# First stage of a two-layer trunk: x first, a smaller first modulation, and a fixed order of issue

## The chip, the cores and the metric

The kernel runs on one NeuronCore of one Trainium2 chip. The metric is the device time of one execution in microseconds (us); a lower time is better. Five kinds of work appear in the profile: PE (TensorE, matrix products, with its weight loads listed as PEld), DVE (VectorE), ACT (ScalarE), POOL (GpSimd) and SP (SyncE), which here issues all transfers between the chip's main memory (HBM) and the on-chip memory (SBUF). PE writes its results to PSUM, from which DVE and ACT read them.

## The reference, cut to what matters

The input `x` has 1024 tokens of 1024 channels, `c` is one conditioning vector. There are two layers, each of the form

```
mod = silu(c) @ ada_w[l] + ada_b[l]
shift, scale, gate = split(mod, 3)
h = rms_norm(x, norm_g[l]) * (1 + scale) + shift
x = x + gate * mixer(h)
```

with `rms_norm(x, g) = x * rsqrt(mean(x * x) + 1e-6) * g` over the channels of a token. The first layer's mixer begins with a projection `h @ w_in` into 3072 channels: q, k, v and a gate of a differential attention, and `x_b` and a gate of a recurrent unit that starts with a convolution of `x_b` along the tokens. The second layer is a neighbourhood attention. A final norm follows.

The change touches only the beginning: the modulation of layer 0, its `rms_norm`, `h`, and the first three slabs (128 output channels each) of the projection.

## The kernel before, in words

**Layout.** Channels lie on the 128 partitions and tokens along the free dimension, so `x` is eight chunks `k` of 128 channels by 1024 tokens. The tokens are worked in two halves `hf` of 512. `half(k, hf)` is one such tile, 128 x 512, 256 KB.

**Exact products.** A product of two 32-bit operands is made of three matmuls: each operand is split into a high part and a remainder (`whi`, `wlo` for a weight slab, `ahi`, `alo` for `h`), and hi·hi, lo·hi and hi·lo are added up in PSUM. A weight slab `i` is a tile `raw` of 512 KB; `split_next` (L159) copies it on ACT into `whi` (L185) and subtracts on POOL for `wlo` (L186), and then loads the next slab (`load_next`, L151).

**The stage before the change** (L503 to L608) does this:

- `squares(hf)` (L516) loads the eight tiles of one half of x, squares them on ACT, some on DVE, and sums the squares over the channels on PE with a matrix of ones (`ss_add`, L366). Each sum is four narrow matmuls, 32 columns of PE each, one for every 128 tokens.
- `mod_first(g)` (L266) loads the modulation weights of two chunks of channels (group `g` of four; eight tiles of 256 KB), sums them on PE with silu(c) as the weight (`sums`, again four narrow matmuls a tile), copies the row on ACT (L296), turns it into a column with a small matmul (L298), and makes `gain` (1 + scale times the norm's gain) and the shift on DVE (L302, L304).
- `scale(hf)` (L539) makes 1/sqrt(mean + eps) on DVE with a bit trick and three Newton steps (`rstd_rows`, L371), spreads it over all partitions with four matmuls (`spread`, L395) and copies it to SBUF on ACT.
- `parts(g, hf)` (L547) calls `make_h` (L399) for two chunks: DVE multiplies x by gain and rstd (L404), ACT adds the shift and rounds to the high part (L405), DVE makes the remainder (L406).
- `products(i, g, hf)` (L553) adds two chunks of one half into slab i's bank: 2 x 3 matmuls of 512 columns (L563, L564, L565). Three slabs, two halves, eight chunks: 144 matmuls in all.
- `small_constants` (L463) is a chain of small DVE steps for the recurrent unit and the attention's lambda, with a Tanh and an Exp on ACT. It is called at the start.

**What sets the order.** A scheduler places each engine's instructions: by their order in the program, among those that it takes to be ready by its own estimates. `tc.high_priority()` moves instructions ahead; `tc.issue_after(ins)` places what is in its block behind `ins` on the same engine's queue, without a wait for its end. Once placed, an engine runs its queue in order, SP's transfers too. In the kernel before, x's first half is loaded first, then the first modulation group, then x's second half, then groups 1, 2 and 3, with the slabs between.

**What follows the stage.** `evac_xb` (L411) copies slabs 0 and 1 from PSUM on ACT; `conv` (L693) works on them on ACT and DVE (L699, L707, L712, L717). `gate_w` (L722) loads and splits the gates' weights (L727 on ACT, L728 on POOL). Meanwhile the job list that begins at L841 runs on PE: half a projection of slab 3, 24 matmuls (`proj`, L201 to L203), and then by turns three gate matmuls on the convolution's result and six matmuls of further projections, with a sigmoid on ACT after every gate.

Of the kernel before, what the change touches and what calls it, by code (L numbers as in the profile page):

```python
# [97 lines left out]
def kernel(ctx, tc, xT, xTp, small, lamp, adaw, tb, w0, gw, wo0, w1, nab, wo1, out):  # L98
# [100 lines left out]

    def mm3(ps, lh, ll, rh, rl, start, stop):  # L200
        T.matmul(ps, lh, rh, start=start, stop=False)  # L201
        T.matmul(ps, lh, rl, start=False, stop=False)  # L202
        state["pe"] = T.matmul(ps, ll, rh, start=False, stop=stop).ins  # L203
# [62 lines left out]
    def mod_first(g, pool, small, c32):  # L266

        ps = ptp.tile([P, HF], F32, tag="pt", name=f"mod{g}")

        def sums(x, w, start, stop):  # L270
            for n in range(4):
                cols = x[:, n // 2, (n % 2) * P:(n % 2 + 1) * P]
                state["modmm"] = T.matmul(ps[32 * n:32 * n + 32, :P], w, cols,
                                          start=start, stop=stop)

        pieces = []
        for k in range(KC):
            where, tag, bufs = pool, "ada", KC
            if g % 2:
                where, tag, bufs = kqp, ("qq0", "qq1", "qlo")[k // 3], 3  # L280
            piece = where.tile([P, 2, 2 * P], F32, tag=tag, name="ada", bufs=bufs)
            src = adaw[0, k * P:(k + 1) * P, :2 * D].rearrange("p (t n) -> p t n", t=2)
            state["ada"] = nc.sync.dma_start(piece[:], src[:, :, 2 * g * P:(2 * g + 2) * P])
            pieces.append(piece)
        if g == 0:
            for k in range(KC):
                sums(pieces[k], c32[:, k, :], k == 0, k == KC - 1)
        else:

            with tc.high_priority():  # L290
                sums(pieces[KC - 1], c32[:, KC - 1, :], True, False)
                with tc.issue_after(state["modmm"].ins):
                    for k in range(KC - 1):
                        sums(pieces[k], c32[:, k, :], False, k == KC - 2)
        row = pool.tile([P, P], F32, tag="mrow", name="mrow", bufs=2)
        A.activation(row[:], ps[:, :P], AF.Copy)  # L296
        pc = ps[:, P:]
        T.matmul(pc[:, :4], row[:], pick[:], start=True, stop=True)  # L298
        m = small.tile([P, 2, 2], F32, tag=f"first{g}", name=f"first{g}", bufs=1)
        gain = small.tile([P, 2], F32, tag=f"gain{g}", name=f"gain{g}", bufs=1)  # L300
        b = sm[:, O_ADAB:O_ADAB + 2 * KC].rearrange("p (t k) -> p t k", t=2)
        V.tensor_tensor(m[:], pc[:, :4].rearrange("p (t j) -> p t j", t=2),  # L302
                        b[:, :, 2 * g:2 * g + 2], ALU.add)
        V.scalar_tensor_tensor(gain[:], m[:, 1, :], 1.0, sm[:, O_NG + 2 * g:O_NG + 2 * g + 2],  # L304
                               ALU.add, ALU.mult)
        for j in range(2):
            first_mod[2 * g + j] = gain[:, j:j + 1], m[:, 0, j:j + 1]
# [58 lines left out]
    def ss_add(ss, sq, start, stop, w=P):  # L366
# [28 lines left out]
    def spread(rr, bc, w=P):  # L395
# [3 lines left out]
    def make_h(l, k, hf, x, bc):  # L399

        g, b = first_mod[k] if l == 0 else (gain1[:, k:k + 1], modc[1][:, k:k + 1])
# [61 lines left out]
    def small_constants(lp):  # L463
# [30 lines left out]
        nc.sync.dma_start(lpv[:], lamp)  # L494
        lv = lpv[:].rearrange("p (a b d) -> p a b d", a=2, b=2)
        V.tensor_tensor(lpm[:], lv[:, :, 0, :], lv[:, :, 1, :], ALU.mult)
        ls = lp.tile([P, 2], F32, tag="ls", name="ls", bufs=1)
        V.tensor_reduce(ls[:], lpm[:], mybir.AxisListType.X, ALU.add)
        A.activation(ls[:], ls[:], AF.Exp)
# [3 lines left out]
    with tc.tile_pool(name="start", bufs=2) as stp, tc.tile_pool(name="ada0", bufs=KC) as adp:  # L503
# [9 lines left out]
        small_constants(stp)  # L513
        nbank = {}
# [65 lines left out]
        with tc.issue_after(state["modmm"].ins):  # L580
            scale(1)
# [915 lines left out]
```

## Time and profile before

| | |
|---|---|
| median of three runs | 1196.18 us (1194.76 to 1197.97) |
| the profiled execution | 1195.79 us, span 1194.1 us |
| PE busy in the span | 1145.0 us (96%) |
| DVE, ACT, POOL busy | 728.8, 566.9, 387.7 us |
| mean granted PE clock | 0.989 of full |

The span runs from the first to the last instruction of the program; the execution's time also holds what lies around it. Times in rows of the profile count from the span's start. A row of the timeline has the start, the duration, the engine, the line of the kernel, the operation, the result and its operands with their sizes, how many instructions it merges and, in brackets, how long the engine had been idle and what ended that. A row of a group has a count, then the busy time and the mean of one in ns, then the idle time before. fp32 products are recorded as more than one matmul record.

### The profile page before, as it was taken

The numbers are of one execution on the slowest core, as the hardware profiler recorded it, in microseconds if no ns is written. First come the engines' busy times: TensorE is split into PE (matmuls) and PEld (weight loads), VectorE is DVE, ScalarE is ACT, GpSimd is POOL, SyncE is SP. The second block draws the span as 40 slices with busy tenths as digits, with TensorE's granted clock in tenths as the row PEclk, the third lists the DMA queues.
The fourth block names the chain that finished last, engine by engine and source line by source line (L and its number), as shares of the span: only waits on it lengthen the run. The fifth ranks groups of instructions, "written<-read, shape, count | busy, mean of one in ns | idle before, by whom it ended". The sixth has DMA issues, their size and how long they took to land.

```text
span 1194.1 us, 19182 instructions
## 1 busy us (share of the span) xinstructions
PE 1145.0 (96%) x7232; PEld 975.6 (82%) x7232; DVE 728.8 (61%) x1414; ACT 566.9 (47%) x1031; POOL 387.7 (32%) x354
## 2 busy tenths in 40 slices
PE   4999999999999999799999999999999999999996
PEld 3788778888777888677879888988998998887896
DVE  6857949499878989767873334233434433555454
ACT  4357586466645557632433444344444434445121
POOL 2124322333333334543413333332333333316200
PEclk8999999999999999899999999999999999999998
DMA  9723132322122110167524433243453543315212
GB/s 331 232 82 118 47 96 71 96 82 76 45 78 63 54 52 22 50 234 247 181 71 118 139 114 86 88 136 106 132 172 88 160 130 113 93 34 163 90 72 71
DMA packets 82045, 132.26 MB, mean 111 GB/s; under 512 B 7584, under 2 KB 48672, under 8 KB 81952
## 3 DMA queue, kind: packets, MB, share of 16 engines
q1 hardware_dynamic: 81952, 131.03, 35.1%
q8 instruction: 57, 0.93, 0.3%
q14 instruction: 36, 0.29, 0.1%
HBM read 110.03 MB, written 14.68 MB: 104 GB/s over the span
## 4 chain that ended last, share of the span: by engine, by line
PE 77%; DVE 12%; ACT 4%; DMA 3%; issue 2%; POOL 1%; SPq 0%; DVEq 0%; ACTq 0%; POOLq 0%
PE pp L201 15%; PE pp L202 15%; PE pp L203 15%; PE no L1333 4%; PE etr L1315 3%; PE v L201 3%; PE v L203 2%; PE v L202 2%; DVE e L927 2%; PE n L659 2%; PE atr L957 2%; PE n L660 2%; PE s L659 1%; PE s L660 1%; POOL wlo L186 1%
## 5 line engine op out<-in xcount | busy, mean ns | idle before, releaser
L201 PE MATMUL pp<-ahi,whi 128*128 128x512 f32 (+1 forms) x1040 | 397.0, 382 | 1.1 <-ACT whi L185 1.0
L203 PE MATMUL pp<-ahi,wlo 128*128 128x512 f32 (+1 forms) x1040 | 394.0, 379 | 2.8 <-POOL wlo L186 2.8
L202 PE MATMUL pp<-alo,whi 128*128 128x512 f32 (+1 forms) x1040 | 394.6, 379 | 0.0
L186 POOL TENSOR_TENSOR wlo<-raw,whi 128x1024 fp32r<-128x1024 f32 x80 | 197.6, 2473 | 257.8 <-ACT whi L185 248.1
L203 PEld LDWEIGHTS pp<-ahi,wlo 128*128 128x128 f32 x1040 | 196.5, 189 | 40.0 <-POOL wlo L186 3.7
L201 PEld LDWEIGHTS pp<-ahi,whi 128*128 128x128 f32 x1040 | 196.6, 189 | 37.2 <-issue 1.9
L202 PEld LDWEIGHTS pp<-alo,whi 128*128 128x128 f32 x1040 | 196.7, 189 | 32.8
L1304 POOL TENSOR_SCALAR e<-e,r 128x288 f32<-128x288 f32 (+1 forms) x128 | 71.2, 568 | 232.6 <-DVE r L1302 232.3
L185 ACT ACTIVATE whi<-raw 128x1024 fp32r<-128x1024 f32 x80 | 84.3, 1056 | 118.0 <-PE pp L202 68.2
L931 ACT ACTIVATE e<-e,nm 128x1024 f32<-128x1024 f32 x64 | 73.6, 1151 | 45.2 <-DVE nm L927 44.9
L1299 ACT ACTIVATE e<-e,nm 128x288 f32<-128x288 f32 (+1 forms) x128 | 72.7, 569 | 42.8 <-DVE nm L1296 42.1
L1321 DVE COPY e<-etr 96x384 f32<-96x384 f32 (+1 forms) x64 | 35.5, 555 | 92.8 <-PE etr L1315 91.2
L1296 DVE CUSTOM_DVE_ANT_0 e<-n,bias 128x288 f32<-128x288 f32 (+1 forms) x128 | 60.6, 504 | 46.0 <-PE n L660 31.9
L1319 ACT ACTIVATE e<-etr 96x384 f32<-96x384 f32 (+1 forms) x64 | 31.3, 489 | 118.5 <-DVE e L1321 118.2
L927 DVE CUSTOM_DVE_ANT_0 e<-s,tb 128x1024 f32<-128x1024 f32 x64 | 77.5, 1219 | 11.3 <-DMA tb<-in_tb_dram 4.6
L948 POOL TENSOR_SCALAR e<-e,r 128x256 f32<-128x256 f32 x32 | 33.6, 1049 | 121.4 <-DVE r L937 59.6
L201 PE MATMUL v<-whi,ahi 128*128 128x256 f32 x256 | 72.2, 282 | 0.0
L203 PE MATMUL v<-whi,alo 128*128 128x256 f32 x256 | 71.9, 281 | 0.0
L202 PE MATMUL v<-wlo,ahi 128*128 128x256 f32 x256 | 71.9, 281 | 0.0
L964 ACT ACTIVATE ath<-atr 128x512 fp32r<-128x512 f32 x64 | 37.6, 596 | 46.0 <-PE atr L957 45.4
L659 PE MATMUL s<-ks,qq 128*128 128x512 f32 x128 | 52.8, 413 | 3.1 <-DVE nm L927 3.1
L1067 ACT ACTIVATE sq<-xh 128x512 f32<-128x512 f32 (+1 forms) x40 | 21.7, 544 | 71.2 <-DVE xh L1062 69.4
(207 smaller groups left out, 2038.5 us busy)
## 6 DMA issues: line engine op xcount, KB each, us to landing
raw<-in_w_dram SPq DMA_DIRECT2D x56, 512.0 KB
ada<-in_adaw_dram SPq DMA_DIRECT2D x96, 256.0 KB
raw<-in_wo_dram SPq DMA_DIRECT2D x24, 512.0 KB
bias<-in_nab_dram SPq DMA_DIRECT2D x64, 144.0 KB
qq<-qq SPq DMA_DIRECT2D x48, 128.0 KB
bias<-in_nab_dram SPq DMA_DIRECT2D x32, 192.0 KB
xT<-in_xT_dram SPq DMA_DIRECT2D x16, 256.0 KB
xh<-in_xTp_dram SPq DMA_DIRECT2D x16, 256.0 KB
```

Of the source, the lines that this page charges most:

```text
L185: A.activation(hi[:], raw[:], AF.Copy)
L186: G.tensor_tensor(lo[:], raw[:], hi[:], ALU.subtract)
L201: T.matmul(ps, lh, rh, start=start, stop=False)
L202: T.matmul(ps, lh, rl, start=False, stop=False)
L203: state["pe"] = T.matmul(ps, ll, rh, start=False, stop=stop).ins
L659: T.matmul(dst, qsel(q[m]), k, start=True, stop=False)
L927: state["dve"] = V.tensor_tensor_reduce(out=e[:], in0=ps[:].rearrange("p a b -> p (a b)"), in1=tbt[h][:, o:o + S], scale=-1.0, scalar=3.0e ...
L931: A.activation(e[:], e[:], AF.Exp, scale=-1.0, bias=nm[:], accum_out=sums[:, m:m + 1])
L1296: state["dve"] = V.tensor_tensor_reduce(out=e[:, m, :n], in0=ps[:, m, :n], in1=bias["now"][m][:, :n], scale=-1.0, scalar=3.0e38, op0=ALU.a ...
L1299: A.activation(e[:, m, :n], e[:, m, :n], AF.Exp, scale=-1.0, bias=nm[:, m:m + 1], accum_out=sums[:, m:m + 1])
L1304: state["pool"] = G.tensor_scalar(e[:, m, :n], e[:, m, :n], r[:, m:m + 1], 0.0, ALU.mult, ALU.add).ins
L1333: T.matmul(po[64 * m:64 * m + 64, b * P:(b + 1) * P], vch[p, b][:kn, j + hf, 64 * m:64 * m + 64], ets[b][:kn, m, j * P:(j + 1) * P], start ...
```

## The change

1. **All of x first.** The transfers are, in order: slab 0, the sixteen tiles of x, the first modulation chunk alone (eight tiles of 128 KB), slab 1, the second chunk alone, slab 2, group 1, group 2, slab 3, group 3. The lambda's input and the gates' weights come after them.
2. **Modulations by one, one and two chunks.** `FirstMod` replaces `mod_first`: group 0 is summed and used in two steps of one chunk (two narrow matmuls a tile instead of four), the others in one step of two chunks.
3. **rstd.** `rstd(hf)` takes a square root on ACT and a reciprocal on DVE, and then one Newton step, in place of the bit trick and three steps.
4. **x times rstd ahead.** `scaled(k, hf)` multiplies x by the spread rstd, read from PSUM, before the modulation is known; the copy of rstd to SBUF is gone. `parts(k)` then makes the high part on ACT as Identity(gain · x + shift), and on DVE h with one two-scalar step and the remainder with a subtraction, for both halves of one chunk.
5. **Order of the products.** Chunks 0 and 1 are first added to slabs 0 and 1; slab 2 is two chunks behind. In each later group the sums of the modulation come first, then one chunk of slab 2, the small matmul, another chunk of slab 2, and then slabs 0 and 1 by turns for the two new chunks. Slab 2's last two chunks come at the end.
6. **Fixed order.** `Pinned` wraps the four engines: what is issued through it stands behind everything traced before on that engine. The splits of slabs 1 and 2 and of the gates' weights are placed behind the latest high parts and modulation loads. `small_constants` is called at the end of the stage.

The core of the diff:

```diff
+    class Pinned:
+        def __init__(self, eng):
+            self.eng = eng
+        def __getattr__(self, name):
+            f = getattr(self.eng, name)
+            return lambda *a, **k: tc.keep_in_program_order(f(*a, **k))
...
+        def sums(self, js, c32, T):
+            ps = self.ps = ptp.tile([P, HF], F32, tag="pt", name=f"mod{self.g}")
+            for k in range(KC):
+                for n, (t, j) in enumerate((t, j) for t in range(2) for j in js):
+                    T.matmul(ps[32 * n:32 * n + 32, :P], c32[:, k, :], self.pieces[k][:, t, j, :],
+                             start=k == 0, stop=k == KC - 1)
...
+        def rstd(hf):
+            v, rr, t = (stp.tile([P, P], F32, tag=g, name=g)[:] for g in ("rs", "rr", "rt"))
+            pA.activation(t, nbank[hf][:, :P], AF.Sqrt, bias=eps[:], scale=1.0 / D)
+            pV.tensor_scalar(v, nbank[hf][:, :P], 1.0 / D, EPS, ALU.mult, ALU.add)
+            pV.reciprocal(rr, t)
+            pV.scalar_tensor_tensor(t, rr, -0.5, rr, ALU.mult, ALU.mult)
+            pV.tensor_tensor(t, t, v, ALU.mult)
+            pV.scalar_tensor_tensor(rr, t, 1.5, rr, ALU.add, ALU.mult)
+            return rr
+        def scaled(k, hf):
+            pV.tensor_tensor(half(k, hf), half(k, hf), nbank[hf], ALU.mult)
+        def parts(k):
+            g, b = first_mod[k]
+            for hf in range(2):
...
+                state["first A"] = pA.activation(hi[:], half(k, hf), AF.Identity, scale=g,
+                                                 bias=b).ins
...
+                pV.tensor_scalar(h[:], half(k, hf), g, b, ALU.mult, ALU.add)
+                state["first V"] = pV.tensor_tensor(lo[:], h[:], hi[:], ALU.subtract).ins
...
+        load_x(0)
+        load_x(1)
+        mod = [FirstMod(0, adp)]
+        mod[0].load((0,), piece)
+        with tc.issue_after(state["ada"]):
+            slab(0)
+        mod[0].load((1,), piece)
...
+        norm_sums(0, psp, "ps")
+        rr = rstd(0)
+        spread(rr, nbank[0], T=pT)
...
+        norm_sums(1, ptp, "pt")
+        for k in range(3):
+            scaled(k, 0)
+        rr = rstd(1)
+        spread(rr, nbank[1], T=pT)
+        scaled(3, 0)
+        scaled(4, 0)
+        scaled(0, 1)
+        mod[0].sums((0,), c32, pT)
+        mod[0].use((0,), adp, stp, pV, pA, pT)
+        parts(0)
+        with tc.issue_after(state["first A"]), tc.issue_after(state["ada"]):
+            slab(1)
...
+        products(0, 0)
+        for k in range(5, KC):
+            scaled(k, 0)
+        scaled(1, 1)
+        mod[0].sums((1,), c32, pT)
+        products(1, 0)
+        mod[0].use((1,), adp, stp, pV, pA, pT)
+        parts(1)
+        products(0, 1)
+        products(1, 1)
...
+        for g in range(1, KC // 2):
+            mod[g].sums((0, 1), c32, pT)
+            products(2, 2 * g - 2)
+            mod[g].use((0, 1), adp, stp, pV, pA, pT)
+            products(2, 2 * g - 1)
...
             for k in (2 * g, 2 * g + 1):
+                parts(k)
...
             for k in (2 * g, 2 * g + 1):
+                for i in range(2):
+                    products(i, k)
+        products(2, KC - 2)
         for i, evac in enumerate((evac_xb(0), evac_xb(1))):
             for hf in range(2):
                 evac(hf, banks[i, hf])
...
+        products(2, KC - 1)
         for hf in range(2):
             evac_v(0)(hf, banks[2, hf])
+        small_constants(stp)
         ahead(3)
```

More of the change, by code (lines that the diff above doesn't have):

```diff
@@ L264 @@
     first_mod = {}
[L266 to L285, printed above, removed]
-            for k in range(KC):
[L287 to L307, printed above, removed]
@@ new lines @@
+        for g in (1, 2):
+            mod.append(FirstMod(g, adp))
+            mod[g].load((0, 1), piece)
+        products(0, 0)
[8 more added lines that the diff above has]
+        products(1, 1)
+        with tc.issue_after(state["first A"]), tc.issue_after(state["ada"]):
+            slab(2)
+        scaled(2, 1)
```

177 lines of the change are left out of this document (90 added, 87 removed).

## The prediction

> **What bounds it now.** The page first, then the engines' busy time in stretches of 3.4 us (columns: stretch, its length, PE's busy time and matmul records, granted clock, DMA share, GB/s; the last row closes a table up to 38.8).
>
> ```profile
> span 1194.1 us, 19182 instructions
> PE 1145.0 (96%) x7232; PEld 975.6 (82%) x7232; DVE 728.8 (61%) x1414; ACT 566.9 (47%) x1031; POOL 387.7 (32%) x354
> ```
> ```profile
> 0.00:3.30 3.30, 0.00 (x0) 1.00 0.32 65
> 3.30:6.70 3.40, 0.00 (x0) 1.00 0.94 325
> 6.70:10.10 3.40, 1.31 (x16) 1.00 1.03 367
> 10.10:13.50 3.40, 1.86 (x32) 1.00 1.06 368
> 13.50:16.90 3.40, 3.29 (x64) 1.00 1.11 358
> 16.90:20.30 3.40, 1.92 (x32) 1.00 1.03 386
> 20.30:23.70 3.40, 1.03 (x5) 1.00 1.06 390
> 23.70:27.10 3.40, 2.61 (x6) 0.50 1.07 366
> 27.10:30.50 3.40, 3.40 (x26) 0.50 1.11 354
> sum 38.80, PE 21.59; mean PE 1.96
> ```
> ```profile
> 38.80:72.40 33.60, 33.59 (x258) 1.00 0.39 126
> ```
>
> PE is the bound nearly everywhere. In the first stage it idles 17 us before 38.8 and partly runs at half clock (0.50 from 23.7); from 38.8 to the stage's end it has no gap. So the change can only win what PE loses before 38.8, and it wins it only if PE is full again earlier, and stays so. The timeline gives the landmarks.
>
> ```profile
> 6.45 0.63 ACT L527 ACTIVATE sq<-xT 128x512 f32<-128x512 f32 x1
> 11.23 1.32 ACT L527 ACTIVATE sq<-xT 128x512 f32<-128x512 f32 x2 [0.72 <-DMA xT<-in_xT_dram]
> 13.15 1.51 PE L368 MATMUL norm<-sq,ones 128*32 128x128 f32 x24 [1.21 <-DVE sq L525]
> 14.72 0.29 DVE L378 TENSOR_SCALAR rs<-norm 128x128 f32<-128x128 f32 x1
> 18.36 1.13 PE L397 MATMUL norm<-rr,sel 128*128 128x128 f32 x8 [1.58 <-DVE rr L384]
> 20.35 0.28 ACT L296 ACTIVATE mrow<-mod 128x128 f32<-128x128 f32 x1 [0.23 <-PE mod L273]
> 21.49 3.52 DVE L404 SCALAR_TENSOR_TENSOR xT<-xT,gain,bcs 128x512 f32<-128x512 f32 x2
> 21.65 2.81 POOL L186 TENSOR_TENSOR wlo<-raw,whi 128x1024 fp32r<-128x1024 f32 x1 [11.97 <-ACT whi L185]
> 25.68 2.69 ACT L527 ACTIVATE sq<-xT 128x512 f32<-128x512 f32 x5
> 33.44 1.95 PE L273 MATMUL mod<-ada,c 128*32 128x128 f32 x64
> 38.81 0.50 PE L563 MATMUL start<-ahi,whi 128*128 128x512 f32 x1 [1.99 <-ACT ahi L405]
> 72.44 0.39 PE L201 MATMUL pp<-ahi,whi 128*128 128x512 f32 x1
> 77.89 0.39 PE L201 MATMUL gate<-xch,gwh 128*128 128x512 f32 x1
> ```
>
> The stage's 144 matmuls end where the next projection begins, at 72.44. From there to 77.89 PE runs that projection's 24 matmuls: 0.227 us each, the price used below. The first gate follows at once, so the convolution of the first slab's result is only just covered. The sums of the second modulation group run at 33.44, near when its data come: by the GB/s rows 1.3 MB had moved by 6.7 and 10.1 MB by 30.5, and the group is complete after 10.0 MB. The changed order moves the same 10.0 MB for it, so those data come no earlier.
>
> **The change, step by step.** I follow the new fixed order until the second group's sums, then add what PE still has to do.
>
> *All of x first.* Small inputs, first slab and x are 4.8 MB, reached at 16.3 by the same rows. The first half's last square started at 11.9, some 1.1 us after its 2.8 MB; so x is there at 17.4 and its last square (0.63) ends at 18.0. Before, the second half's squares began only at 25.7; this is the real gain, some 8 us.
>
> *Sums of squares and rstd.* The 24 records of three tiles took 1.51 us, 0.43 a tile and 0.25 to drain; at full clock a tile is 0.22. The new rstd replaces nine short DVE steps by a square root on ACT, a reciprocal and three steps. Both are in the tail of the kernel, where the longest is the 128x128 one:
>
> ```profile
> L391 ACT ACTIVATE rs<-ssl,eps x3: 313/314/368, 1137.3 to 1184.8; 128x64 f32<-128x64 f32 x2, 128x128 f32<-128x128 f32 x1
> L391 ACT ACT_TABLE_LOAD  x1: 1283/1283/1283, 1135.5 to 1135.5; - x1
> L392 DVE RECIPROCAL rr<-rs x3: 552/553/953, 1137.7 to 1185.1; 128x64 f32<-128x64 f32 x2, 128x128 f32<-128x128 f32 x1
> L404 DVE SCALAR_TENSOR_TENSOR xh<-xh,gain,bc 128x512 f32<-128x512 f32 x16 | 11.2, 737 | 1.8 <-PE bc L397 1.8
> L405 ACT ACTIVATE ahi<-xT,first 128x512 fp32r<-128x512 f32 x16 | 11.1, 724 | 11.4 <-DVE xT L404 11.4
> L717 DVE TENSOR_TENSOR xcl<-xc,xch 128x512 fp32r<-128x512 f32 x4 | 2.6, 687 | 1.2 <-ACT xch L712 1.2
> ```
>
> So 0.37 + 0.95 + 3 x 0.33 + hops = 2.5 us, where from the old one's start (14.7) to the spread (18.4) it was 3.6. If PE has full clock, the sums end at 18.5, rstd at 21.0, its spreading (1.15) at 22.2. If PE is at half clock, as the pace of 0.43 a tile says of the first 17 us (the clock column shows 1.00 there), the first spreading, now queued ahead of the second half's sums, ends near 17.3, and eight tiles of 0.43 then end at 20.8: rstd 23.3, spread 24.4. The table load stands ahead of the first squares, where x is late anyway; it costs nothing as long as squares catch up (five in 2.69, 0.52 apart, against tiles 0.7 apart by the rate).
>
> *One chunk of modulation at a time.* 64 records took 1.95 us, 0.03 apart, but the eight of a spread, of as many columns, 1.13: four narrow products run side by side. With one chunk there are two instead of four, so I take the same 1.95, not half; half is the other bound. The first chunk's sums end at 24.1 (half clock: 26.3). From their end to the first use of the gain it was 20.3 to 21.5, so 1.2.
>
> *Splitting h.* ACT makes the high part (0.72) while DVE makes h and the remainder for both halves in turn. Neither the two-scalar step (0.48 by the nearest row, below) nor the scaling from PSUM (0.74 by L404 on a PSUM operand) stands in the old stage. One after another, 0.77, 0.69, 0.48, 0.69 and hops, DVE's last remainder ends 2.75 after the gain, so six matmuls, worth 1.4, take until 3.0 after it. Then in PE's fixed order: sums of the second chunk 1.9, six matmuls of slab 1 1.4, pick and gain 0.8 (the 1.2 less the copy of the row, which lies under slab 1), again 3.0, and 1.4. The second group's sums start at 24.1 + 1.2 + 3.0 + 1.9 + 1.4 + 0.8 + 3.0 + 1.4 = 36.8; at half clock 39.0. Scaling made ahead from PSUM costs DVE 16 x 0.6 more, but behind waits for modulations; I cost it at nothing, and 0.6 each where that cover is gone.
>
> *Transfers and the slabs' splits.* The first group's eight loads of 256 KB become sixteen of half the size; a chunk of 1.05 MB is 2.9 us at 366 GB/s, or 5.7 if a half load costs a whole one. The first chunk is then there at 20.3 to 23.1, wanted at 22.2; the second, behind slab 1, at 24.6 to 31.8, wanted at 28.3 to 30.6: nothing, with up to 1 us of stall at the far end. On SP the third group's loads wait for the first group's buffers, free after its second sums; slab 3, the fourth group and the gate weights queue behind, wanted only after 45. Slab 1's split follows the first high parts on ACT (1.05) and takes POOL up to 2.8, until 5.3 after the gain, wanted at 5.1: nothing. The two L404 at 21.49 took 3.52 beside POOL's 2.81; of the sixteen L404 xh on a PSUM operand none is stretched (737 on average). The scaling reads PSUM, so I let POOL hold only the steps with SBUF operands.
>
> *The rest.* 120 matmuls x 0.227 = 27.2, three sums 5.7, picks at most 0.75 (part of the 1.2), and in each group a stall of 0.75: after the gain PE has six matmuls to run (1.4) and needs the last remainder at 2.75. Together 35.9. The stage ends at 72.7, or 74.9 with the slow front: +0.3 to +2.5 against 72.44. I take 2.5, since the front of the old stage was slow in just these microseconds.
>
> *The clock.* The stretch with 1.03 us of work was followed by 0.50, the one with 1.92 not. In the new order the stretch up to 23.7 has about 0.9 us of work, so half clock may come back: 1.5 to 2.2 us more, an end near 77. The Trainium skill (TensorE: Matmul & The Clock Gate, Part 1) has PE fall to half after a window without activity and recover after one busy window; by that rule PE would keep full clock here and the end stays at 74.9 or below. The trace differs, since 1.03 us of work did not save it and 2.61 did not release it.
>
> *End of stage and the convolution.* These rows are the junction, and one row for the two-scalar step.
>
> ```profile
> 49.02 1.77 POOL L728 TENSOR_TENSOR gwl<-gwr,gwh 128x512 fp32r<-128x512 f32 x1 [17.27 <-ACT gwh L727]
> 49.57 1.77 DVE L404 SCALAR_TENSOR_TENSOR xT<-xT,gain,bcs 128x512 f32<-128x512 f32 x1
> 64.53 1.06 ACT L185 ACTIVATE whi<-raw 128x1024 fp32r<-128x1024 f32 x1 [0.81 <-PE start L565]
> 66.11 1.25 ACT L699 ACTIVATE xc<-xb,sm 128x1024 f32<-128x1024 f32 x1
> 67.39 8.94 DVE L707 SCALAR_TENSOR_TENSOR xc<-xb,sm,xc 128x1022 f32<-128x1022 f32 x5 [8.32 <-ACT xc L699]
> 68.39 3.02 POOL L186 TENSOR_TENSOR wlo<-raw,whi 128x1024 fp32r<-128x1024 f32 x1 [0.32 <-ACT whi L185]
> 76.25 1.29 DVE L717 TENSOR_TENSOR xcl<-xc,xch 128x512 fp32r<-128x512 f32 x2
> 81.13 0.48 DVE L334 TENSOR_SCALAR macc<-ada,ctmp 128x512 f32<-128x512 f32 x1
> ```
>
> Before, slab 0 was done at 64.45 (its buffers released L185 at 64.53), 8.0 us before the stage's end, and its convolution reached the gates 13.4 us later, DVE being held while POOL ran. In the new loop slabs 0 and 1 alternate to the last chunk; after slab 0's last product only 18 matmuls remain, 4.1 us. With the 24 of the next projection the gates are wanted 9.5 us after slab 0: 3.9 too early by the old rows. Two of the five DVE steps belong to the other convolution (2 x 1.28) and may fall behind. I take 2.0, between 0 (other matmuls are queued ahead of the gates) and 3.9. The gate weights' split on POOL, now behind the last high part, holds DVE as at 49.57 (1.77 for 0.75): up to 1.0 on the last remainder; I take 0.4. The exponential of the lambdas now needs a table load there, 1.28 by the row and hidden if ACT still waits for slab 0; I put it at 0. The Trainium skill (ScalarE: Activation LUTs, What ACT_TABLE_LOAD costs) counts 2.66 us with the drain; by it 1.4 more could show at this place, and the front is unchanged.
>
> Sum: 2.5 + 2.0 + 0.4 = +4.9. After the junction gates, sigmoids and scans follow PE, so I carry it to the end. The profiled execution took 1195.79, 0.4 below the median of 1196.18: **1195.8 + 4.9 = 1200.7**.
>
> **Rivals.** *Faster: the second group's sums start when their data are there.* Place: PE at 33.0 instead of 36.8; the end is 33.0 + 35.9 = 68.9, -3.5, and if DVE is then ahead the three stalls go too (-2.25), while slab 0's junction takes some back: 1191. It decides from 3.8 us saved on the chain above. For it: half a modulation at half price would give 1.9 of them. Against: every other step has its row. *Same:* full clock throughout (+0.3), gates hidden behind other matmuls: 1196.5. For it: PE is 96% busy and a list of ready work stands behind the gates; against: the half pace before 16.9. *Worse:* half clock returns at 23.7 (+4.6), the junction costs its whole 3.9 and the remainder 1.0: 1205.3. The row with 1.03 speaks for it. *It doesn't do what it says:* the order holds only for wrapped calls, and the small constants, some 30 DVE steps, are free; if they drop into the junction the gates wait longer still, which I count with worse.
>
> **How the numbers follow.** Forecast 45%, its own range 1198 to 1204; worse 15%; same 28%; faster 12%. A difference under 0.3%, 3.6 us, can't be told from none. Slower by more: 45 + 15, less 2 for the forecast's lower edge, 58%; within 30%; faster 12%. Range 1194 to 1206: it holds same, forecast and worse, and leaves out faster and what lies past 1206.
>
> **What would show it.** Squares of the second half from about 12 and its last near 17.4 (step one); sums of the second group at 37 to 39 (the chain; at 33 the forecast falls); the first L201 of the next projection near 75; a gap of PE before the first gate that waits for L717 or its operands; a granted clock of 0.50 before 30. If PE shows no gap before the first gate, or the stage ends before 70, I am wrong.

## The result: 1.35% slower, and where the time went

The changed kernel took 1213.95 us (median of four, 1211.70 to 1215.57), the kernel before 1196.97 beside it. The ratio is 1.0135, with a 95% interval of 1.0110 to 1.0159. The profiled execution took 1214.02 us; its page begins with the span and the busy time of each engine:

```profile
span 1212.3 us, 19226 instructions
PE 1158.5 (96%) x7234; PEld 983.3 (81%) x7234; DVE 729.4 (60%) x1419; ACT 570.9 (47%) x1036; POOL 387.0 (32%) x354
```

The span is 18.2 us longer. PE is busy for 13.5 us more with almost the same matmuls (two records more), so a part of the loss is not waiting but slower work. The timeline of PE in the changed kernel has the same landmarks as the one shown of before (what goes through `Pinned` has the one line L208):

```profile
17.84 3.64 PE L208 MATMUL norm<-sq,ones 128*32 128x128 f32 x64
24.14 1.16 PE L208 MATMUL norm<-rr,sel 128*128 128x128 f32 x8 [2.65 <-DVE rr L208]
25.22 3.47 PE L208 MATMUL mod<-ada,c 128*32 128x128 f32 x32
33.44 3.01 PE L208 MATMUL mod<-ada,c 128*32 128x128 f32 x32
43.44 1.95 PE L208 MATMUL mod<-ada,c 128*32 128x128 f32 x64
...
81.26 0.39 PE L211 MATMUL pp<-ahi,whi 128*128 128x512 f32 x1
...
91.69 0.80 PE L211 MATMUL gate<-xch,gwh 128*128 128x512 f32 x1 [4.83 <-ACT xch L774]
```

The second group's sums begin at 43.44 (before: 33.44), the next projection at 81.26 (72.44), the first gate at 91.69 (77.89). So 13.8 of the 18.2 us have been lost when the first gate runs. The table of PE's waits between 12 and 97 us (line, releaser, total, times, longest) names the places:

```profile
PE norm L208 <- DVE rr L208: 5.4, 2, 2.7
PE gate L211 <- ACT xch L774: 4.8, 1, 4.8
PE start L208 <- ACT ahi L208: 2.6, 2, 1.3
```

In the front PE waits twice for rstd and twice for a high part; at the junction it waits once, for the convolution. What the waits do to the clock is in PE's stretches of 3.41 us (stretch, length, busy time and records, granted clock, DMA share, GB/s):

```profile
22.02:25.43 3.41, 1.29 (x12) 1.00 1.05 238
25.43:28.84 3.41, 3.27 (x32) 0.50 1.03 362
28.84:32.26 3.42, 1.90 (x7) 1.00 1.07 343
32.26:35.67 3.41, 3.11 (x24) 0.50 0.15 41
35.67:39.08 3.41, 2.67 (x22) 1.00 0.83 265
...
86.87:90.28 3.41, 0.00 (x0) 1.00 0.00 0
90.28:93.69 3.41, 2.00 (x4) 0.50 0.00 0
93.69:97.11 3.42, 3.42 (x9) 0.50 0.38 108
```

The first chunk's sums (25.22) and the second's (33.44) each fall into a stretch at half clock, which the wait before has brought about; the first gates fall into two. (The second half's sums at 17.84 also run at half pace, 64 records in 3.64 where the second group's take 1.95, although the clock column shows 1.00 there.) At the junction the twelve matmuls from 91.69 to 97.21, where the timeline shows the next at full pace, took 5.5 us instead of 12 x 0.227 = 2.7: another 2.8. Why the gates were late is in ACT's and DVE's timeline there:

```profile
77.41 1.04 ACT L185 ACTIVATE whi<-raw 128x1024 fp32r<-128x1024 f32 x1
78.77 1.06 ACT L185 ACTIVATE whi<-raw 128x1024 fp32r<-128x1024 f32 x1 [0.32 <-PE start L208]
79.74 2.04 ACT L424 ACTIVATE xb<-start 128x512 f32<-128x512 f32 x4
81.65 1.11 ACT L431 ACTIVATE vT<-start 128x512 f32<-128x512 f32 x2
82.60 2.41 ACT L761 ACTIVATE xc<-xb,sm 128x1024 f32<-128x1024 f32 x2
83.92 7.25 DVE L769 SCALAR_TENSOR_TENSOR xc<-xb,sm,xc 128x1022 f32<-128x1022 f32 x6 [6.04 <-DMA raw<-in_w_dram]
90.09 0.60 ACT L424 ACTIVATE xb<-pp 128x512 f32<-128x512 f32 x1 [5.08 <-DVE xc L769]
90.59 1.99 ACT L774 ACTIVATE xch<-xc 128x1024 fp32r<-128x1024 f32 x2
91.67 2.50 DVE L779 TENSOR_TENSOR xcl<-xc,xch 128x512 fp32r<-128x512 f32 x4 [0.50 <-ACT xch L774]
```

Slab 0's last product is behind PE at 77.13, and slab 1's follows 1.4 us later. ACT first splits two weight slabs (L185), then evacuates slabs 0 and 1 and the value slab, and makes the first `xc` only at 82.60. DVE does the six steps of both convolutions by turns, so the first convolution is whole after five of them, at 90.0 (83.92 + 7.25, less 1.2 for the sixth). ACT then evacuates a tile of the next projection (90.09) before it rounds the result (L774). (The bracket at 83.92 names a transfer, but DVE starts 0.04 after the end of the first `xc`, at 82.60 + 1.28.)

Against the forecast of +4.9 the 18.2 us are, by these rows: stage end 8.8 (forecast 2.5), wait before the first gate 10.43 - 5.45 = 5.0 (2.0, and 0.4 for the gate weights' split), half clock behind it 2.8 (0), and 1.6 more behind it. Two later stretches of half clock were one step of 3.41 us longer than before (from 373.59, shown in the last section, and from 551.08); across them the same matmuls of the two timelines move apart by 1.4 and 1.2, and other places give back 1.0.

### The profile page after: what moved, and what is told of

It reads as the page before. It is cut to its first block, busy times and chain, and to the rows that moved or that the text cites. A ratio compares the mean times of both kernels' runs of the same rounds, so it can differ in the third digit from the quotient of the medians.

```text
span 1212.3 us, 19226 instructions
## 1 busy us (share of the span) xinstructions
PE 1158.5 (96%) x7234; PEld 983.3 (81%) x7234; DVE 729.4 (60%) x1419; ACT 570.9 (47%) x1036; POOL 387.0 (32%) x354
## 4 chain that ended last, share of the span: by engine, by line
PE 75%; DVE 10%; DMA 5%; issue 4%; ACT 4%; POOL 2%; SPq 0%; DVEq 0%; POOLq 0%; ACTq 0%
PE pp L211 15%; PE pp L213 15%; PE pp L212 15%; PE no L1396 3%; PE etr L1378 3%; PE v L211 2%; PE v L213 2%; PE v L212 2%; DVE e L990 2%; PE n L721 2%; DMA ada<-in_adaw_dram 2%; PE atr L1020 2%; PE n L722 2%; PE s L721 1%; PE s L722 1%
## 5 line engine op out<-in xcount | busy, mean ns | idle before, releaser
L211 PEld LDWEIGHTS pp<-ahi,whi 128*128 128x128 f32 x1040 | 197.7, 190 | 37.8 <-issue 1.9
L185 ACT ACTIVATE whi<-raw 128x1024 fp32r<-128x1024 f32 x80 | 84.3, 1056 | 115.9 <-PE pp L212 65.0
```

Source lines behind the costliest of these rows:

```text
L185: A.activation(hi[:], raw[:], AF.Copy)
```

## Experiments

Each is compared with the kernel before on the same chip; single executions of one kernel differ (the kernel before ran from 1191.6 to 1203.6 us in all), so the ratios count; by their intervals, two ratios less than some 0.35% apart are hardly told from each other. No kernel leaves out anything that is computed. "Next projection" and "first gate" are read from each profile's timeline of PE, one execution each; the place of the clock's steps alone moved such a reading by 0.7 us (last section).

| kernel | next projection | first gate | ratio (95% interval) |
|---|---|---|---|
| before | 72.44 | 77.89 | 1 |
| changed | 81.26 | 91.69 | 1.0135 (1.0110 to 1.0159) |
| e4 no fixed order | 70.23 | 80.68 | 1.0019 (1.0001 to 1.0036) |
| e13 PE free | 74.33 | 84.67 | 1.0079 (1.0052 to 1.0107) |
| e15 PE, DVE free | 73.00 | 83.44 | 1.0051 (1.0024 to 1.0079) |
| e16 PE, ACT free | 74.39 | 84.77 | 1.0076 (1.0047 to 1.0104) |
| e5 one line moved | 77.92 | 88.36 | 1.0086 (1.0056 to 1.0115) |
| e1 PE filled | 84.88 | 95.30 | 1.0121 (1.0092 to 1.0151) |
| e11 waits filled | 76.75 | 87.18 | 1.0103 (1.0059 to 1.0148) |
| e9 before, x first | 78.77 | 84.21 | 1.0028 (1.0006 to 1.0049) |
| e14 no fixed order, x later | 74.41 | 84.85 | 1.0060 (1.0039 to 1.0081) |
| e10 no fixed order, pair first | 72.31 | 82.75 | 1.0056 (1.0030 to 1.0083) |
| e2 convolution first | 82.00 | 89.44 | 1.0076 (1.0048 to 1.0103) |
| e3 other order of products | 80.27 | 85.92 | 1.0052 (1.0030 to 1.0075) |
| e7 e4 and e2 | 70.36 | 77.72 | 0.9989 (0.9964 to 1.0013) |
| e12 e4, e2 and e3 | 70.09 | 75.53 | 0.9969 (0.9949 to 0.9989) |

### Is it the fixed order?

```diff
-            return lambda *a, **k: tc.keep_in_program_order(f(*a, **k))
+            return f
```

> The changed kernel without its fixed order: the same operations, the order of each engine left to the planner's own costs. Theory (the fixed order itself costs little; data, clock and junction cost): stage end within 2 us of 81.26, the wait before the first gate 4 to 6 us, time 1211 to 1216. Rival (the fixed order makes PE wait in front of ready work, as between 28.7 and 42): the second group's sums start at 40 or earlier and the time is below 1210.

The rival came, and by more than it asked. The same operations without the fixed order took 1200.35 us. PE's timeline of that kernel:

```profile
19.54 2.00 PE L299 MATMUL mod<-ada,c 128*32 128x128 f32 x31
24.21 1.28 PE L406 MATMUL norm<-rr,sel 128*128 128x128 f32 x8
70.23 0.39 PE L211 MATMUL pp<-ahi,whi 128*128 128x512 f32 x1
80.68 0.79 PE L211 MATMUL gate<-xch,gwh 128*128 128x512 f32 x1 [4.84 <-ACT xch L774]
```

The second group's sums began before 40, as the rival asked. The first chunk's sums run at 19.5, ahead of the second half's spreading, because nothing but their weights is needed; in the fixed order they run at 25.2, behind it. The next projection begins 11.0 us earlier than in the changed kernel and 2.2 earlier than before. The wait for the convolution is the same 4.8, so it is a loss of its own.

Which engine's order? First PE's alone was freed (`T` in place of `Pinned(T)`), then PE's with DVE's, then PE's with ACT's.

> The changed kernel with the fixed order taken from PE alone; ACT, DVE and the loads keep theirs. Theory (the loss of the fixed order lies in PE's queue: sums of modulations that are ready stand behind rstd, and the first slab's remainders ahead of other ready products): next projection at 70 to 72.5, second group's sums begin at 32 to 35, time 1199 to 1202.5, as without any fixed order (1200.35). Rival (the order on DVE and ACT costs as much, the first gain waiting behind scaling steps): next projection at 75 to 79, time 1205 to 1211.

> The changed kernel with the fixed order taken from PE and DVE; ACT and the loads keep theirs. Freeing PE alone brought the next projection to 74.33, freeing all to 70.23, with the same order of loads; 4.1 us lie in ACT's or DVE's order. Theory (DVE: the scaling steps stand ahead of the first gain and hold it until 26.4, and ahead of the second's): first gain near 23 to 24, next projection at 70 to 71.5, time 1199 to 1202.5. Rival (ACT: its squares and high parts keep a worse order): next projection at 73.5 to 75, time 1204 to 1207.

> The changed kernel with the fixed order taken from PE and ACT; DVE and the loads keep theirs. Theory (DVE's order holds the first gain): next projection stays at 73.5 to 75, time 1204 to 1207. Rival (ACT's order is what costs): next projection at 70 to 71.5, time 1199 to 1202.5.

Freeing PE gives 6.9 of the 11.0 us: the next projection falls between e13's theory and its rival, the time (1205.79) into the rival. In e13 the first gain is made at 26.21, behind three scaling steps, after which DVE still waits 0.6 for PE's small matmul; without any fixed order (e4, second fence) it is made at 24.00:

```profile
23.39 2.02 DVE L208 TENSOR_TENSOR xT<-xT,norm 128x512 f32<-128x512 f32 x3
26.01 0.16 DVE L208 TENSOR_TENSOR first<-mod,sm 128x2 f32<-128x2 f32 x1 [0.60 <-PE mod L307]
26.21 0.16 DVE L208 SCALAR_TENSOR_TENSOR gain<-first,sm 128x1 f32<-128x1 f32 x1
```
```profile
24.00 0.15 DVE L313 SCALAR_TENSOR_TENSOR gain<-first,sm 128x1 f32<-128x1 f32 x1
```

But freeing DVE as well gives only 1.3 more, which single readings and the ratios hardly tell from nothing, and freeing ACT as well gives nothing: neither DVE's order nor ACT's alone is the other 4.1 us. 2.8 us appear only when all are free, though the loads go out in the same order in e13, e15 and e4; to which engine they belong is open.

### One line of the fixed order

```diff
         rr = rstd(1)
+        mod[0].sums((0,), c32, pT)
         spread(rr, nbank[1], T=pT)
...
-        mod[0].sums((0,), c32, pT)
```

> The changed kernel, its fixed order kept, with one line moved: the sums of the first chunk's modulation stand on PE ahead of the second half's spreading of rstd instead of behind it, so they run while DVE makes rstd. They need only the modulation weights and the condition. Theory (the fixed order itself is what costs: it puts the first modulation behind both norms, though it depends on neither; without the fixed order its sums ran at 19.5 and the next projection began at 70.2): the first gain comes near 26.5 instead of 29.8, the second group's sums start at 39 to 40.5 instead of 43.44, the next projection begins at 77 to 78.5 instead of 81.26, the wait before the first gate stays 4.8; time 1208.5 to 1211. Rival (this place costs nothing, because the scaling steps on DVE or the second chunk's weights are late next): second group's sums within 1 us of 43.44, time 1212.5 to 1215.

In PE's timeline the sums now lie under the making of rstd, and the rest moves up:

```profile
20.59 1.91 PE L208 MATMUL mod<-ada,c 128*32 128x128 f32 x32
23.42 1.16 PE L208 MATMUL norm<-rr,sel 128*128 128x128 f32 x8 [0.92 <-DVE rr L208]
77.92 0.39 PE L211 MATMUL pp<-ahi,whi 128*128 128x512 f32 x1
```

That one line is worth 3.3 us at the stage's end, as the theory had it.

### The clock in the front

Extra 128x128 products fill PE's waits. The first try put ten of them ahead of all sums:

```diff
+        def warm(n):
+            for _ in range(n):
+                pT.matmul(banks[0, 0][:, :P], state["sel"][:, 0, :], state["sel"][:, 1, :],
+                          start=True, stop=True)
...
+        warm(10)
         norm_sums(0, psp, "ps")
         rr = rstd(0)
+        warm(8)
...
         rr = rstd(1)
+        warm(8)
```

> The changed kernel with idle PE time of the front filled: 37 extra 128x128 products of the selection matrix with itself, into a bank that the first slab's product overwrites; nothing that is computed changes. Ten stand ahead of the first sums, one between each two tiles of them, eight in each of the two waits for rstd, four behind the first pick. Theory (the half clock costs the front about 4.5 us: 1.7 in the second half's sums of 3.64, 1.7 in the first chunk's 3.47, 1.1 in the second chunk's 3.01): the granted clock shows no 0.50 between 25 and 36, the second half's sums end near 18, those of the first chunk take 1.8 to 2.0, the second group's sums start at 37 to 39 instead of 43.44, and the next projection begins at 74.5 to 77 instead of 81.26. The wait before the first gate stays near 5 us. Time 1207 to 1209.5. Rival (the chain through ACT and DVE and the arrival of the modulation weights set the front, the clock is only a symptom): sums get shorter but the second group's sums start within 1 us of 43.44, time 1213 to 1215.

Their operand was made late by POOL: the table of waits has "PE start L208 <- POOL sel L136: 9.8", so all sums of squares stood behind them and the first spreading came at 23.57 instead of 15.87. From there to the second group's sums it took 23.4 us instead of 27.6. The kernel was no test of the whole time, so the second try filled only the waits, with five, eight and four products.

> The changed kernel with its fixed order, and extra 128x128 products only where PE waits in the front: five in the first wait for rstd, eight in the second, four behind the first pick (none ahead of the sums, which was what held the first such kernel up). Nothing that is computed changes. Theory (half clock in the front costs 4.2 us, as the stretch from the first spreading to the second group's sums shrank from 27.6 to 23.4 there): no 0.50 before 38, the second half's sums take 2.0 to 3.0, each chunk's sums 1.95, second group's sums at 39 to 40.5 instead of 43.44, next projection at 77 to 78.5, the wait before the first gate stays 4.8; time 1208.5 to 1211. Rival (the chain through ACT and DVE sets the front): second group's sums within 1 us of 43.44 and time 1212.5 to 1215.

PE's timeline:

```profile
17.82 1.99 PE L208 MATMUL norm<-sq,ones 128*32 128x128 f32 x64
23.56 1.94 PE L208 MATMUL mod<-ada,c 128*32 128x128 f32 x32
29.95 1.94 PE L208 MATMUL mod<-ada,c 128*32 128x128 f32 x32
38.89 1.95 PE L208 MATMUL mod<-ada,c 128*32 128x128 f32 x64
76.75 0.39 PE L211 MATMUL pp<-ahi,whi 128*128 128x512 f32 x1
```

No stretch of the front shows 0.50, the two chunks' sums take 1.94 instead of 3.47 and 3.01, and the second group's sums and the next projection begin 4.5 us earlier. With no other step touched, that is what the slow pace cost the front. It has two parts: 1.65 us lie in the second half's sums (1.99 instead of 3.64), ahead of the first stretch with 0.50; the other 2.9 lie between the first chunk's sums and the second group's (15.3 instead of 18.2 us) and are the price of the two slow stretches. (It overlaps with the line moved in e5, which fills the same wait with useful work.)

### Which part of the change is worth what

The kernel before with all of x loaded first:

```diff
-            for k in range(KC):
-                state["x"] = nc.sync.dma_start(half(k, hf), xT[k * P:(k + 1) * P,
-                                                               hf * HF:(hf + 1) * HF])
+            if hf == 0:
+                for h in range(2):
+                    for k in range(KC):
+                        state["x"] = nc.sync.dma_start(
+                            half(k, h), xT[k * P:(k + 1) * P, h * HF:(h + 1) * HF])
```

> The kernel before with one part of the change: all sixteen loads of x stand ahead of the first modulation's weights; nothing else is touched. Theory (x first gains nothing by itself, since the second group's weights come no earlier and PE is full from there): second half's squares end near 18, the first modulation's sums end 3 to 6 us later than before, near 25 to 27, the second group's sums start at 33 to 34.5, the next projection begins within 1.5 us of 72.44; time 1195 to 1198.5. Rival (x first is what makes the free order's stage end at 70.2): next projection at 70 to 71, time 1192 to 1194.5. Rival on the other side (the first products wait for the later weights and the half clock stays longer): next projection at 74 to 77, time 1198.5 to 1202.

The changed kernel without fixed order, x's second half behind the first chunk's weights:

```diff
-        load_x(1)
         mod = [FirstMod(0, adp)]
         mod[0].load((0,), piece)
+        with tc.issue_after(state["ada"]):
+            load_x(1)
```

> The changed kernel without its fixed order and with one transfer order turned back: x's second half is loaded behind the first chunk's modulation weights instead of ahead of them; all else as in the changed kernel without its fixed order (next projection at 70.23, first gate 80.68, 1200.35). Theory (x first is no gain of its own, as it was none in the kernel before: the weights that set the pace come no earlier, and PE is full from 30 on either way): the first gain comes 1 to 3 us earlier, the second half's rstd 2 to 3 us later, the next projection at 69.5 to 71.5, the wait before the first gate stays 4.8; time 1199 to 1202. Rival (x first is the real gain of the change, as the blind working had it, some microseconds of it even with one chunk at a time): next projection at 72 to 75, time 1202.5 to 1206.

The same without fixed order, the first two chunks' modulation as one pair (`load`, `sums` and `use` with `(0, 1)`):

> The changed kernel without its fixed order and with the first two chunks' modulation made as one group, as before the change. Theory (one chunk at a time brings the first gain 2.9 us earlier, 1.05 MB at 366 GB/s, but PE catches up by the second group, whose weights set the pace): first gain near 25 to 26 instead of 23, next projection at 70 to 71.5, time 1199 to 1202.5. Rival (the early first products are worth their whole 2.9 us): next projection at 72.5 to 74, time 1202.5 to 1205.

My theory fell all three times. x first alone delays the kernel before: the next projection begins at 78.77, 6.3 later, past the bad end of the rival, though the span is only 4.6 longer (1198.7). In the new order without fixing, x first helps: taking it back costs 4.2 us at the stage's end and 0.41% in the ratio, and taking back the single chunks costs 2.1 there and 0.37% in the ratio. How it helps is open: in e14 the first `gain` was expected earlier and is made at 25.78, later than the 24.00 of e4. The parts need each other: with x first the first `gain` waits for later weights (27.40 in e9 and 27.36 in e10, against 21.30 in the kernel before), and the halved first chunk brings a part of that back (24.00).

### The junction

Precedence for the first slab's evacuation and its convolution:

```diff
-                evac(hf, banks[i, hf])
+                with tc.high_priority() if i == 0 else nullcontext():
+                    evac(hf, banks[i, hf])
...
-        conv(0)
+        with tc.high_priority():
+            conv(0)
```

> The changed kernel with one thing about the junction: the evacuation of the first slab and its convolution are given precedence, so that ACT makes the first xc before it evacuates the second slab and the value slab, and DVE does the three steps of the first convolution before the second's. Theory (the wait before the first gate is 5.0 us because the two convolutions take turns on DVE, six steps of 1.2 in a row, and ACT puts four evacuations ahead of the first xc; and that wait brings the half clock of 90.3 to 97.1, 2.8 us): stage end unchanged near 81.3, first xc near 80.8, its last DVE step ends near 85.8, first gate 86.7 to 87.3, no 0.50 in that place; time 1205.5 to 1207.5. Rival (the wait only moves: the second convolution, the remainder of the first or the gate weights come late instead): the sum of PE's waits between 86 and 130 falls by less than 2 us, time 1211 to 1214.

The time came as expected, but not the way there. DVE and POOL in that kernel, and the first gate:

```profile
82.28 7.16 DVE L770 SCALAR_TENSOR_TENSOR xc<-xb,sm,xc 128x1022 f32<-128x1022 f32 x4 [3.65 <-ACT xc L762]
```
```profile
79.76 4.76 POOL L186 TENSOR_TENSOR wlo<-raw,whi 128x1024 fp32r<-128x1024 f32 x2 [3.35 <-ACT whi L185]
```
```profile
89.44 0.50 PE L211 MATMUL gate<-xch,gwh 128*128 128x512 f32 x1 [1.83 <-ACT xch L775]
```

Four steps take as long as six did in the changed kernel: the first begins while POOL splits a slab until 84.52, and lasts 3.3 us (7.16 less three of the usual 1.28). So 1.8 us of the wait stay. No half clock follows; the clock's stretch that holds this wait (85.54 to 88.95) still has 2.07 us of work. From the end of the stage the gate comes 7.4 us later instead of 10.4; with the half clock gone, 5.8 us are won there.

The other way is cover: `products` of slab 2's last four chunks at the end, each group's sums inside the products before.

```diff
...
+        for i in range(2):
+            products(i, KC - 2)
+            products(i, KC - 1)
+        for k in range(4, KC - 1):
+            products(2, k)
...
```

> The changed kernel with another fixed order from the second group on: each group's sums stand inside the products of the group before, and the third slab's products of the last four chunks are kept for the end, so that 36 matmuls (8.2 us) instead of 18 follow the last product of the first slab. Front, ACT's and DVE's order of the convolutions stay. Theory (slab 0 ends too late for the convolution to be covered, and each group stalls for its last remainders): the second group's sums still start near 43.4, the stage ends at 80 to 81.5, the first gate follows the next projection with a wait of 0 to 2 us, no half clock behind it; time 1205 to 1207.5. Rival (DVE is the bound of the second half of the stage, 5 us of work a group): the stage ends at 83 or later and the time is 1209 to 1213 in spite of the covered convolution.

PE's timeline of that kernel at the junction:

```profile
80.27 0.39 PE L211 MATMUL pp<-ahi,whi 128*128 128x512 f32 x1
...
85.92 0.50 PE L211 MATMUL gate<-xch,gwh 128*128 128x512 f32 x1
```

The first gate comes 5.65 us after the next projection, whose 24 matmuls take 5.45: no wait worth the name, although the two convolutions still take turns: 36 matmuls behind the first slab's end are cover enough, as the kernel before had it. The stage's end moves by only 1.0. The time, 1202.81, is 2 us better than the theory's range.

### All of it

e7 has the edits of e4 and of the convolution's precedence, e12 also the other order of the products (there as the order of writing).

> The changed kernel without its fixed order, and with precedence for the first slab's evacuation and convolution. Theory (fixed order and junction are separate losses that add): next projection at 70 to 71, first gate some 7.4 us later at 77 to 78.5 instead of 80.68, no 0.50 behind it; time 1193 to 1196, at or below the kernel before. Rival (the planner, given other precedence, moves the wait to the second convolution or the gate weights): the wait before the first gate falls but later waits take it back, time 1198.5 to 1201.

> The changed kernel without its fixed order, with the other order of the products as its order of writing (36 matmuls behind the first slab's last) and with precedence for the first evacuation and convolution: all that helped, together. Theory (the 1.6 us that PE still waited for the first gate go, since 8.2 us of products now cover the convolution, and stage end stays at 70.4): next projection at 70 to 71, first gate 5.4 us later at 75.5 to 76.5 with no wait, time 1193.5 to 1196, 1 to 3 us below the kernel before. Rival (ACT's and DVE's work of the last group, or the gate weights, come too late for an earlier gate): waits of 1.5 us or more between 70 and 130, time 1196 to 1198.

PE's timeline of e12 at the junction:

```profile
70.09 0.39 PE L211 MATMUL pp<-ahi,whi 128*128 128x512 f32 x1
...
75.53 0.40 PE L211 MATMUL gate<-xch,gwh 128*128 128x512 f32 x1
```

Fixed order and junction add: at the first gate e4 wins 11.0 us, e2 2.3, and e7, which has both, 14.0. Without both the change is back at the time of before (1196.85, 0.9 above the range of e7's theory). With the other order of the products too (e12), the first gate runs 2.4 us earlier than before and the time is 1194.12 us: 0.31% below the kernel before, with an interval that stays below 1.

## Why the prediction was wrong

**Right: direction and chain.** I forecast slower, and followed the queue in the right order. x was complete when said (its last squares ended at 17.4), rstd took 2.65 to 2.74 (forecast 2.5, hops included), a chunk's sums with two narrow products cost what four cost (1.94 against 1.95 at full clock, e11), and transfers cost PE nothing (the one wait of 0.3 that the table of waits puts down to a load ends at 32.72, when DVE has just finished a remainder). The exponential's table load (1.28 at 73.93) cost nothing, since ACT had no work behind it until 77.30. That x first is the real gain is shown only without the fixed order and with single chunks: 4.2 us of the 8 (e14); in the kernel before it is a loss (e9).

**The clock.** The forecast took half clock for the front's beginning and put its return into the rival "worse" with 15%. It returned in 25.43 to 28.84 and 32.26 to 35.67. The forecast's chain with the slow front (half pace up to the second half's sums, full-clock prices from the spreading on) was: sums from 24.4, second group's sums at 39.0. Measured: start 25.2 (+0.8), first chunk's sums 3.47 instead of 1.9 (+1.6), first split and products 3.6 instead of 3.0 (+0.6), second chunk's sums 2.9 to the next product instead of 1.9 (+1.0), the rest +0.4: 43.44, 4.4 later. I had a row that said this (1.03 us of work in a stretch, then 0.50), counted 0.9 us of work up to 23.7, and still left it out of the sum. Of the 4.5 us that e11 wins, 2.9 are this return; the other 1.65 lie in the second half's sums, whose half pace the forecast had priced. So the step that failed here is the return of the half clock, which the sum put at nothing; the other 1.5 of the 4.4 are small sizes, the late start above all. The Trainium skill (TensorE: Matmul & The Clock Gate, Part 1) has the clock fall after a window without activity; here stretches with 1.29 and 1.90 us of work were followed by 0.50, so a forecast by that rule would have made the front too fast as well.

**The rest of the stage.** 35.9 us were forecast from the second group's sums on, 37.8 were measured. 120 matmuls at 0.227 and three sums at 1.89 make 32.9; waits for remainders, the small matmuls and restarts took 4.9 instead of 3.0.

**The junction.** The step "two of the five DVE steps belong to the other convolution (2 x 1.28) and may fall behind" failed: they did not fall behind, they took turns, and ACT put two weight splits and four evacuations in between. 5.0 us were measured where I took 2.0 from a range to 3.9. The upper bound was a misreading as well: 13.4 us after slab 0 is when PE came to the gate, not when the convolution was ready. The old kernel's rounded result was there at 75.31, 10.9 us after the slab:

```profile
74.25 1.06 ACT L712 ACTIVATE xch<-xc 128x1024 fp32r<-128x1024 f32 x1 [3.68 <-DVE xc L707]
```

In the changed kernel it took 14.5 us from 77.1, and the gates were wanted after 9.5: the 5.0. From the slab to the first `xc` it is 5.5 us instead of 1.7 (64.45 to 66.11), and two steps of the other convolution add 2.4; beside POOL's splits two of the old steps had taken 2.5 more (1.77 and 3.30 instead of 1.28 each), and that is gone here. That the two slabs alternate to the last chunk stood in the prediction, but not what it does to the order on ACT and DVE. (The gate weights' split did hold a step of DVE, 1.52 instead of 0.54 at 74.43, but PE waited for that last remainder only 0.2 longer than for the others; 0.4 were forecast.)

**What was missing.** The forecast carried its sum from the junction to the end unchanged. But a wait of 5 us also brought two stretches of half clock, 2.8 us. The row with 1.03 us could have warned of it.

**The rivals.** "Worse" had the place and the two mechanisms, at 1205.3; it was the nearest, and too small. "Faster" needed the second group's sums at 33.0; they ran at 43.44, and a chunk's sums did not get cheaper by half. "Same" hung on full clock and on other matmuls ahead of the gates, and neither was there. The small constants did not drop into the junction: their chain ended at 13.7, and only the lambda's short steps ran at 76.66 to 77.88, when DVE had nothing else to do until 83.92. That the fixed order itself was the larger loss (11 us at the stage's end) was none of my cases: I priced the order as written and did not ask what the scheduler would do with the same operations.

## What to carry to other kernels

Before fixing an order by hand, ask of each instruction in the queue what it really depends on: whatever is ready and stands behind something that waits can be lost twice, as idle time and as half clock afterwards. Price a wait of PE together with the slow stretch that can follow it: here one followed the waits of 2.7 and 4.8 us, and none the waits of 1.6 and 1.8 before the first gate (e7, e2); several short waits together brought another (1.90 us of work between 28.84 and 32.26). When a loop is changed so that two results end together, look at the engines that take them over: whoever needs the first one gets it late.

## What was not expected of the hardware

In each profiled execution the changes of the granted clock lie on a grid of 3.41 us from the first one. In the changed kernel the stretches that begin at 32.26 and 90.28 lie 2 and 19 steps behind the one at 25.43 (25.43 + 2 x 3.413 = 32.26; 25.43 + 19 x 3.413 = 90.28). So the same wait can cost one step or two. The same place of the attention, in stretches of PE, before and in the changed kernel:

```profile
354.82:358.23 3.41, 0.45 (x5) 1.00 0.25 102
358.23:361.64 3.41, 3.24 (x8) 0.50 0.02 5
361.64:365.06 3.42, 3.42 (x19) 1.00 0.49 128
```
```profile
370.18:373.59 3.41, 0.85 (x8) 1.00 0.27 108
373.59:377.00 3.41, 2.76 (x7) 0.50 0.02 5
377.00:380.42 3.42, 3.42 (x10) 0.50 0.30 77
```

Inside a slow stretch 3.24 us of work restored the clock and 2.76 did not. Ahead of one, the work in a single stretch doesn't decide it: in the changed kernel 1.29 us and 1.90 did not hold the clock and 2.67 did (35.67 to 39.08), but 1.84 held it too (158.55 to 161.96), and in e7 2.41 did not (21.31 to 24.72).

A shift of a few microseconds moves every later wait on that grid. The front shows what that can do: up to 74 us the changed kernel and e2 run the same instructions in the same order on PE, ACT, DVE and the loads, and the first spreading starts at 15.87 and 15.82. But e2's grid lies 1.3 us earlier, three stretches of its front are slow instead of two (from 24.10, 30.92 and 41.16), and its stage ends 0.7 us later. I take this for a reason why one kernel's whole executions differ by several microseconds (e3: 1196.8 to 1206.0), but no run changed the grid alone over a whole execution, so that is argued, not shown.
